# Second-layer values of two heads by seven block products, with their weight sums made ahead and the value step one head later

## The chip, the cores and the metric

One core of one Trainium2 chip runs the whole program once. The metric is the device time of one execution in microseconds (us), taken as the median of the runs shown. All matmuls run on TensorE (PE). VectorE (DVE) and ScalarE (ACT) evict and transform, GpSimd (POOL) does a few additions and issues the transfers of the prepared weights, SyncE (SP) issues most other transfers. PSUM holds eight banks, four for products (`mmt`) and four for everything else (`axt`).

## The reference

Two decoder layers over 528 tokens (16 learned ones and 512 real ones) of width 1024. The first layer is an mLSTM with an RG-LRU, the second differential attention; each is followed by a squared-ReLU MLP of width 4096. The change is in the second layer's attention:

```python
def _diff_attn(hn, w_in, lam_vecs, subln, w_out, lambda_init):
    q, k, v = _split(hn @ w_in, C_SPLITS)       # 8 heads; q, k: 2 x 64 each, v: 128
    ...
    q = _partial_rope(q, cos, sin) * (C_QK_DIM ** -0.5)
    k = _partial_rope(k, cos, sin)
    ...
def _diff_attend(qb, q_pos, kh, vh, k_pos, lam):
    s = jnp.einsum('bhcqd,bhckd->bhcqk', qb, kh)
    p = jax.nn.softmax(jnp.where(mask, s, -jnp.inf), axis=-1)
    pd = p[:, :, 0] - lam * p[:, :, 1]
    return jnp.einsum('bhqk,bhkv->bhqv', pd, vh)
```

Here `hn` is the RMS-normed residual; each head's output is normed again over its 128 columns and goes through `w_out`.

## The kernel before

Activations lie with the features on the partitions and the 528 tokens along the free dimension, cut into eight k blocks of 128 features. Every fp32 operand is split into a high and a low half (`split`: ACT rounds, DVE subtracts), and each product is made of three matmuls: high by high, low by high, high by low. A weight unit is 128 x 1024, eight blocks of 128 x 128. A full product of a unit is 48 matmuls of 264 columns (two banks), or 24 of 512 columns (one bank) where only the real tokens are wanted (`unit_mm`, `cuts`).

The MLPs already make some products in the way that the change brings to the values: `pair_mm` takes two weight units and two token halves as a 2 x 2 by 2 x 2 block product with seven instead of eight block products, on sums of weight blocks (`sums`, `rest`) and of input blocks (`pair_x`). Its three banks are X, Y and Z.

The second layer runs head by head (`attend`): a query product (512 columns), a key product, a value product, each evicted with the row scale `rstd` that the norm leaves out of its inputs. `norm_x` only multiplies by the norm weights, splits, and squares (`norm_sq`). Between them stand the steps of the earlier head (`attn_steps`): `s0` to `s3` are the scores and softmax of four query blocks, `t0` to `t3` the transposes of the probabilities, `v` the transposes of the values into token-major form, `o` the product of probabilities and values, `f` the norm of the head's output into `co`. `SLOTS` is an order written out by hand: slot 0 stands ahead of a head's query product, 1 in its middle, 2 after it, 3 and 4 the same for the key, 5 in the middle of the value product; a prime means one head further back. The framework then schedules all instructions on its engines' queues by that order as priority (`soon` and `now` raise it) and by what is ready, so instructions of several steps and products interleave; it also places the tiles in memory by their lifetimes.

After the last head, the out-projection first multiplies heads 0 to 5 and then heads 6 and 7 (`OUT_K`), with the last heads' steps between its blocks.

The second layer's weights (`AHEAD`: 24 units of query, key and value, 8 of the out-projection) are prepared during the first MLP: `make_ahead` runs every five steps of that MLP's 225 (`STAGE`), fetches half units into `ra` through POOL's queue, splits them two turns later and stores the halves in DRAM (`parts`). In the second layer `emit_load` loads them with SP into three buffers (tag `w`).

## Time and profile before

| | |
|---|---|
| median of 3 runs (lowest to highest) | 1402.62 us (1402.36 to 1403.05) |
| the profiled execution, its span | 1402.5 us, 1400.6 us |
| first layer up to its MLP | 0 to about 444 us |
| first MLP | to 799.5 us |
| second layer's heads | 800 to 990 us |
| out-projection and last heads' steps | 990 to 1048 us |
| second MLP and the output | to 1400.6 us |

A row of the table of stretches gives, for each engine, busy us and the number of instructions, then the granted TensorE clock as a share of full speed (1.00 throughout these stretches), the mean share of the 16 DMA engines and GB/s. A row of the timeline or of the chain that ended last gives the start, the duration and what ran; in brackets stands how long the engine was idle before it, and what ended that. A row of the groups gives busy us and the mean ns of one, and the idle time ahead of them.

### The profile page before, as it was taken

To read this page: it belongs to the slowest core of one execution; us is meant where nothing else is said; L and a number is where in the kernel's file an instruction comes from. 1 tells how busy PE (TensorE), PEld (TensorE's weight loads), DVE (VectorE), ACT (ScalarE), POOL (GpSimd) and SP (SyncE) were. 2 spreads that over 40 slices of the span, in tenths; PEclk is the share of its full clock that TensorE was granted. 3 is DMA by queue.
4 is the path that set the end of the run, shared out by engine and by line. 5 is a ranking of instruction groups with operands and counts; after the bars stand their busy time and mean duration, and the time that the engine had idled before them with its cause. 6 is when DMAs were issued, how large, how long until landed. Compare 5 with 4: busy or idle time off the path is not lost.

```text
span 1400.6 us, 25665 instructions
## 1 busy us (share of the span) xinstructions
PE 1391.1 (99%) x10195; PEld 1324.6 (95%) x10195; DVE 1014.5 (72%) x1836; ACT 764.5 (55%) x1345; POOL 178.7 (13%) x270
## 2 busy tenths in 40 slices
PE   9999999999999999999999999999999999999998
PEld 9999999999999999999999999999887889889986
DVE  6867764757845998888886457878778977777752
ACT  7465844647524565656554336566666554454542
POOL 3000001010012034345430300000011000000001
PEclk9999999999999999999999999999999999999999
DMA  7342324223224369889872266555442333233231
GB/s 227 127 121 84 90 76 128 67 71 105 76 91 129 100 234 355 302 312 318 304 266 85 113 218 198 176 181 166 153 164 65 134 118 118 75 110 105 76 121 45
DMA packets 70068, 210.18 MB, mean 150 GB/s; under 512 B 12570, under 2 KB 14631, under 8 KB 69948
## 3 DMA queue, kind: packets, MB, share of 16 engines
q1 hardware_dynamic: 52732, 154.98, 34.6%
q0 software_dynamic: 15360, 50.34, 9.7%
q10 hardware_dynamic: 1856, 3.21, 0.7%
q8 instruction: 80, 1.31, 0.4%
q14 instruction: 40, 0.33, 0.1%
HBM read 162.11 MB, written 35.71 MB: 141 GB/s over the span
## 4 chain that ended last, share of the span: by engine, by line
PE 80%; ACT 1%; DVE 0%; issue 0%; ACTq 0%
PE mw L997 23%; PE mm L426 21%; PE mpY L345 8%; PE mpX L345 5%; PE mpZ L345 5%; PE mn L997 4%; PE mf L1342 3%; PE mo L1306 3%; PE po L1266 2%; PE pt L1242 1%; PE mm L440 1%; PE psc L1208 1%; PE psc L1207 1%; PE pnum L718 1%; PE pv L1188 0%; PE pss L694 0%
## 5 line engine op out<-in xcount | busy, mean ns | idle before, releaser
L241 ACT CAST wh<-raw 128x1024 fp32r<-128x1024 f32 x139 | 145.4, 1048 | 258.6 <-PE mw L997 82.0
L997 PE MATMUL mw<-al,wh 128*128 128x264 f32 (+1 forms) x704 | 221.2, 314 | 0.0
L997 PE MATMUL mw<-ah,wh 128*128 128x264 f32 (+1 forms) x704 | 221.0, 314 | 0.0
L997 PE MATMUL mw<-ah,wl 128*128 128x264 f32 (+1 forms) x704 | 220.9, 314 | 0.0
L162 DVE TENSOR_TENSOR wl<-raw,wh 128x1024 fp32r<-128x1024 f32 (+1 forms) x138 | 164.5, 1193 | 52.1 <-ACT wh L241 50.2
L997 PEld LDWEIGHTS mw<-ah,wl 128*128 128x128 f32 x704 | 132.4, 188 | 8.3
L997 PEld LDWEIGHTS mw<-ah,wh 128*128 128x128 f32 x704 | 132.4, 188 | 7.3
L997 PEld LDWEIGHTS mw<-al,wh 128*128 128x128 f32 x704 | 132.3, 188 | 7.3
L1041 DVE TENSOR_TENSOR h<-mw,h 128x264 f32<-128x264 f32 (+1 forms) x176 | 87.4, 497 | 22.0 <-PE mw L997 21.5
L521 POOL TENSOR_TENSOR nsq<-nsq 128x528 f32<-128x528 f32 (+1 forms) x28 | 42.2, 1508 | 356.0 <-ACT nsq L519 355.5
L345 PE MATMUL mpX<-xp,A_h 128*128 128x264 f32 (+1 forms) x416 | 77.3, 283 | 0.0
L345 PEld LDWEIGHTS mpX<-xp,A_h 128*128 128x128 f32 x416 | 65.1, 188 | 1.1
L345 PE MATMUL mpX<-xp,A_l 128*128 128x264 f32 (+1 forms) x208 | 58.9, 283 | 0.0
L162 DVE TENSOR_TENSOR al<-rt,ah 128x528 fp32r<-128x528 f32 (+1 forms) x64 | 46.0, 719 | 17.1 <-ACT ah L165 16.5
L280 ACT CAST S_h<-sums 128x1024 fp32r<-128x1024 f32 x26 | 27.3, 1051 | 38.3 <-issue 12.6
L1355 POOL TENSOR_TENSOR zg<-z,gfr 128x512 f32<-128x512 f32 x4 | 5.2, 1294 | 328.2 <-DVE z L1349 328.2
L1007 ACT ACTIVATE rt<-rt 128x528 f32<-128x528 f32 (+1 forms) x64 | 40.7, 638 | 9.9 <-DVE rt L1028 8.7
L162 DVE TENSOR_TENSOR ral<-ra,rah 128x512 fp32r<-128x512 f32 x64 | 43.7, 682 | 2.6 <-DMA ra<-wu 1.3
L1220 ACT ACTIVATE e<-e,mx 128x144 f32<-128x144 f32 (+3 forms) x64 | 32.8, 513 | 20.0 <-DVE mx L1212 19.7
L165 ACT CAST ah<-rt 128x528 fp32r<-128x528 f32 (+1 forms) x64 | 40.1, 626 | 1.5
L352 DVE TENSOR_TENSOR hh<-mpZ,hh 128x264 f32<-128x264 f32 (+1 forms) x52 | 22.1, 426 | 25.7 <-PE mpZ L345 25.6
L165 ACT CAST rah<-ra 128x512 fp32r<-128x512 f32 x64 | 37.9, 613 | 3.0 <-DMA ra<-wu 2.8
(941 smaller groups left out, 4378.3 us busy)
## 6 DMA issues: line engine op xcount, KB each, us to landing
raw<-wu SPq DMA_DIRECT2D x139, 512.0 KB, 3.6
rawp<-wu SPq DMA_DIRECT2D x26, 1024.0 KB, 6.4
ra<-wu POOLq DMA_DIRECT2D x64, 256.0 KB, 5.6
h<-hT SPq DMA_DIRECT2D x15, 264.0 KB, 4.9
st<-rh SPq DMA_DIRECT2D x16, 132.0 KB, 4.1
st<-rh ACTq DMA_DIRECT2D x16, 132.0 KB, 4.2
kz<-rl SPq DMA_DIRECT2D x16, 132.0 KB, 5.5
st<-rh SPq DMA_DIRECT2D x16, 128.0 KB, 3.6
```

Of the source, the lines that this page charges most:

```text
L162: eng.tensor_tensor(out=o, in0=a, in1=b, op=ALU.subtract)
L165: nc.scalar.copy(hl[0][:, sl], src)
L241: nc.scalar.copy(wh, raw)
L345: nc.tensor.matmul(st[b][:, :hv], ww[:, cc], xx, start=st[b, "n"] == 0, stop=k == 3 and j == 2, skip_group_check=True)
L426: nc.tensor.matmul(p[:, :m], w[:, c], xx[:, s:s + m], start=(k == 0 and j == 0), stop=(k == KB - 1 and j == len(terms) - 1))
L521: state["kz"] = nc.gpsimd.tensor_tensor(out=fin[0][:, lo:], in0=fin[0][:, lo:], in1=sq[:, lo:], op=ALU.add)
L997: nc.tensor.matmul(ps, w[ww], x[xx][:, tk], start=k == j == 0, stop=k == len(ws) - 1 and j == 2)
L1007: nc.scalar.activation(out=t[:, cols], in_=t[:, cols], func=AF.Square)
L1041: nc.vector.tensor_tensor(out=hf, in0=ps, in1=hf, op=ALU.add)
L1220: nc.scalar.activation(out=e[:, s0:s0 + m], in_=e[:, s0:nk] if last else d[:, :m], func=AF.Exp, scale=-1.0 if last else 1.0, bias=top, acc ...
L1306: nc.tensor.matmul(ps, w[ww][:, b], co[k][xx][:, NM:], start=(k == ks[0] and j == 0), stop=(k == ks[-1] and j == 2))
L1342: nc.tensor.matmul(pss[n][:, :m], a[k][aa][:, tk], w[k][ww][:, f0:f0 + m], start=(k == 0 and i == 0), stop=(k == KB - 1 and i == 2))
```

## The change

The values of two heads are made together, as in the MLPs: seven block products on the two units' blocks and the two token halves. The even head makes four of them (a copy of the first product, two sums, and the first half of its own values), the odd head three. The even head's values are complete only in the odd head, so the step `v` moves one head later; `SLOTS` becomes four orders, for the first two heads, even and odd heads, and the end. The row scale moves from the eviction of the product to the value transposes (`rsV`, rstd transposed through DRAM).

`norm_pairs` takes the place of `norm_x` and also makes the input sums. The blocks lie apart in memory now, so a query product is cut into 248 and 264 columns (two banks).

The weight sums are made in `make_ahead`: 76 half units are split instead of 64 and 16 sums are added; up to two jobs a turn, stores issued in the same turn, `STAGE` up to step 218. The loads move to four buffers shared with the MLP (tag `v`). Besides, small constants move into one tile, one explicit activation table preload is dropped, and in the last recurrent pair a squaring moves from DVE to ACT.

```diff
-SLOTS = ("t2' s0", '', "t1' t3'", '', "o'", "s2 s1 v f' s3 t0")
+SLOTS = (("t2' s1'", '', "v' t3'", "t1' s0 o' t0", '', "s2 s3 f'"),
+         ("t2' s1'", 's0', "t3'", "v' s2 t1' o' t0", '', "f' s3"),
+         ("s1' t2' s0", '', "v' t3'", "t1' o'", 't0', "s2 f' s3"),
+         ("s1' s0", "t2'", "t3'", "v' t1' o'", 's2 t0', "f' s3"))
...
-STAGE = set(range(8, 184, 5))
+STAGE = set(range(8, 220, 5))
...
+        for _u in AHEAD:
+            if _u in V_PAIR:
+                jobs += [("s2", _u), ("s3", _u), ("a0", _u), ("a1", _u), ("s0", _u), ("s1", _u), ("d", _u)]
+            elif all(_u - _p not in (1, 4, 5) for _p in V_PAIR):
+                jobs += [(0, _u), (1, _u)]
...
-            cuts = [(lo, n)] if n <= 512 else [(0, HV), (HV, HV)]
+            cuts = [(lo, n)] if n <= 512 and not isinstance(x[0][0], tuple) else [(lo, HV - lo), (HV, HV)]
...
+            def even(mid):
...
+                ps = product("X", A, 0, B11)
+                with soon():
+                    nc.scalar.copy(h["a"], ps)
+                ps = product("Y", S, 1, N2)
+                with soon():
+                    nc.vector.tensor_tensor(out=h["b"], in0=ps, in1=h["a"], op=ALU.add)
+                mid()
+                ps = product("Z", S, 0, N1)
+                with soon():
+                    nc.vector.tensor_tensor(out=h["c"], in0=ps, in1=h["b"], op=ALU.add)
+                ps = product("X", A, 1, B21)
+                with soon():
+                    nc.scalar.copy(v[0][:, s1], ps)
...
+            def odd(mid):
...
+                ps = product("Y", U, 0, T3)
+                with soon():
+                    nc.vector.scalar_tensor_tensor(out=v[1][:, s2], in0=ps, scalar=-1.0, in1=h["c"], op0=ALU.mult,
+                                                   op1=ALU.subtract)
+                ps = product("Z", U, 1, B22, mid)
+                with soon():
+                    nc.vector.tensor_tensor(out=v[0][:, s2], in0=ps, in1=h["c"], op=ALU.add)
+                ps = product("Y", D, 0, T4)
...
+        def norm_pairs(h, gc):
...
+                for o, hh, g, m in ((n1, h[:, k, :HV], pc(gc + k), b12), (t3, h[:, k + 1, HV:], pc(gc + k + 1), b12),
+                                    (n2, h[:, k, :HV], gneg[:, k:k + 1], t3), (t4, h[:, k + 1, :HV], gneg[:, k + 1:k + 2], n2)):
+                    nc.vector.scalar_tensor_tensor(out=o, in0=hh, scalar=g, in1=m, op0=ALU.mult, op1=ALU.subtract)
+                for o, m in ((hi.a[:, 4:7], b[:, 0:3]), (hi.b, t4)):
+                    nc.scalar.copy(o, m)
+                for o, m, i in ((lo.a[:, 4:7], b[:, 0:3], hi.a[:, 4:7]), (lo.b, t4, hi.b)):
+                    sub(nc.vector, o, m, i.bitcast(F32))
...
-                    if pr == 3:
-                        nc.vector.tensor_tensor(out=d["a2"], in0=d["a"], in1=d["a"], op=ALU.mult)
-                    else:
-                        nc.scalar.activation(out=d["a2"], in_=d["a"], func=AF.Square)
+                    nc.scalar.activation(out=d["a2"], in_=d["a"], func=AF.Square)
...
-            vr = sc("vr1")
-            steps.append(attn_steps(hd, rot, vr))
-            ps = unit_mm(u + 2, x, mid=lambda: slot(hd, 5))
-            with soon():
-                for p, tk in ps:
-                    nc.vector.tensor_tensor(out=vr[:, tk], in0=p, in1=rstd[:, tk], op=ALU.mult)
+            mid = lambda: slot(hd, 5)
+            if hd % 2 == 0:
+                vals.append(values_in_pairs(u_qkv(hd, 2), xp))
+                steps.append(attn_steps(hd, rot, vals[-1][0][0]))
+                vals[-1][1](mid)
+            else:
+                steps.append(attn_steps(hd, rot, vals[-1][0][1]))
+                vals[-1][2](mid)
...
+                    for j, (s0, sz) in enumerate(KBLK):
+                        i, c = j // 4, slice((j % 4) * P, (j % 4 + 1) * P)
+                        nc.scalar.activation(out=vt[0][i][:sz, c], in_=pvs[i][:sz, c], func=AF.Copy, scale=rsV[:sz, j:j + 1])
+                        nc.vector.scalar_tensor_tensor(out=vt[1][i][:sz, c], in0=pvs[i][:sz, c], scalar=rsV[:sz, j:j + 1],
+                                                       in1=vt[0][i][:sz, c].bitcast(F32), op0=ALU.mult, op1=ALU.subtract)
```

More of the change, by code (lines that the diff above doesn't have):

```diff
@@ L39, with u_qkv, __init__, at @@
 U_QKV = 129
-U_OUT1 = 153
-U_MLP1 = 161
-N_UNIT = 225
+U_OUT1 = 161
+U_MLP1 = 169
+N_UNIT = 233
+def u_qkv(hd, w):
+    return U_QKV + 8 * (hd // 2) + 4 * (hd % 2) + w
+V_PAIR = [u_qkv(hd, 2) for hd in range(0, 8, 2)]
+class Blocks:
+    def __init__(self, a, b):
+        self.a, self.b = a, b
+    def at(self, i):
+        return self.a[:, i, :] if i < 7 else self.b
 PLAN = """
@@ L57 @@
 N_S = 31
-AHEAD = range(129, 161)
+AHEAD = range(U_QKV, U_MLP1)
 N_W = 4
@@ new lines, in trunk, with half, job, add @@
+        n_job = [0]
+        got, made, sums = {}, [], {}
+        def half(c):
+            return slice(c * 512, c * 512 + 512)
+        def job(j, u):
+            if j in (0, 1):
+                return got.pop((u, j))[1], u, j
+            r = {v: got[u, v][1] for v in range(4) if (u, v) in got}
+            def add(k, a, b):
+                o = sc("rs_")[:, :512]
+                nc.vector.tensor_tensor(out=o, in0=a, in1=b, op=ALU.add)
+                if k > 1:
+                    sums[u, k] = o
+                return o
+            if j == "s2":
+                return add(2, r[3], r[2]), u + 1, 0
+            if j == "s3":
+                return add(3, sums.pop((u, 2)), r[0]), u + 1, 1
+            if j == "a0":
+                return r[0], u, 0
+            if j == "a1":
+                return got.pop((u, 1))[1], u, 1
+            if j == "s0":
+                del got[u, 0], got[u, 2]
+                return add(0, r[0], r[2]), u + 4, 0
+            if j == "s1":
+                return add(1, sums.pop((u, 3)), state.pop(("r1", u))), u + 4, 1
+            return got.pop((u, 3))[1], u + 5, 0
@@ L255, in make_ahead, with here @@
         def make_ahead():
             state["turn"] = state.get("turn", 0) + 1
+            def here(j, u):
+                need = {"s2": (2, 3), "s3": (0,), "a1": (1,)}.get(j, (j,) if j in (0, 1) else ())
+                return all((u, v) in got and got[u, v][0] <= state["turn"] - LAG for v in need)
+            n = 0
+            while jobs and n < 2 and here(*jobs[0]):
+                j, u = jobs.pop(0)
+                if j == "a1":
+                    state["r1", u] = got[u, 1][1]
+                raw, to, c = job(j, u)
+                hl = sc("rah", F32R), sc("ral", F32R)
+                split(hl, raw, slice(0, 512))
+                made.extend((part[:, half(c)], t) for part, t in zip(parts[to - AHEAD[0]], hl))
+                n += 1 if j in (0, 1) else PJOB
@@ L260, in make_ahead @@
                 nc.gpsimd.dma_start(out=part, in_=t[:, :512].bitcast(F32))
-            while came and came[0][0] <= state["turn"] - LAG:
-                _, i, c, raw = came.pop(0)
-                hl = sc("rah", F32R), sc("ral", F32R)
-                split(hl, raw, slice(0, 512))
-                made.extend((part[:, c], t) for part, t in zip(parts[i - AHEAD[0]], hl))
-            if ahead:
-                i = ahead.pop(0)
-                for c in (slice(0, 512), slice(512, 1024)):
+            for _ in range(2):
+                if fetch and len(got) < CAP:
+                    u, v, src, c = fetch.pop(0)
                     raw = sc("ra")[:, :512]
-                    nc.gpsimd.dma_start(out=raw, in_=wu[seq[i]][:, c])
-                    came.append((state["turn"], i, c, raw))
+                    nc.gpsimd.dma_start(out=raw, in_=wu[seq[src]][:, half(c)])
+                    got[u, v] = (state["turn"], raw)
         todo = []
@@ L843, in out_gate @@
             nc.scalar.activation(out=so[c], in_=so[c], func=AF.Sigmoid)
-        sp = cp.tile([P, 8], F32, name="sp")
-        spn = cp.tile([P, 8], F32, name="spn")
+        sp = small(8)
+        spn = small(8)
         def lru_consts():
@@ L1074, in trunk @@
         mlp(0, 0, "m", between)
-        while ahead or came or made:
+        while jobs or made:
             make_ahead()
-        assert not (ahead or came or made)
+        assert not (jobs or made or got or sums)
         dump("h2", h)
-        x, terms1 = norm_x(h, C_NMIX1, 0, "d")
-        tb = [sc(f"tb{i}") for i in range(2)]
+        xp, terms1 = norm_pairs(h, C_NMIX1)
+        xq = [tuple((t, o) for t in hl) for hl in xp for o in (0, 2)]
+        tb4 = big.tile([P, 2, T], F32, tag="tb", name="tb", bufs=1)
+        tb = [tb4[:, i] for i in range(2)]
+        vals = []
+        rrow2 = dr.tile([1, T], F32, name="rrow2")
+        rsV = small(5)
         for i in range(2):
-            nc.sync.dma_start(out=tb[i], in_=rope[i])
+            load(tb[i], rope[i])
         lvt = cp.tile([1, 4, 64], F32, name="lvt")
@@ L1119, in slot @@
         def slot(hd, i):
-            for s in SLOTS[i].split():
+            for s in SLOTS[0 if hd < 2 else 1 if hd > 7 else 2 + hd % 2][i].split():
                 g = hd - 1 - s.count("'")
```

127 lines of the change are left out of this document (98 added, 29 removed).

## The prediction

> **What bounds the kernel now.** I read the page's busy shares first, then the table of stretches, then the chain that ended last, then single instructions. In the fences the first number of a timeline or chain row is its start in us.
>
> ```profile
> span 1400.6 us, 25665 instructions
> PE 1391.1 (99%) x10195; PEld 1324.6 (95%) x10195; DVE 1014.5 (72%) x1836; ACT 764.5 (55%) x1345; POOL 178.7 (13%) x270
> core 0: us, PE busy (x) PEld busy (x) DVE busy (x) ACT busy (x) POOL busy (x), PEclk, DMA share, GB/s
> 460.00:799.50 339.50, 339.50 (x2789) 339.50 (x2788) 278.40 (x444) 187.52 (x278) 111.51 (x196) 1.00 0.71 246
> 862.00:887.40 25.40, 25.40 (x180) 23.75 (x179) 20.23 (x63) 16.22 (x47) 0.00 (x0) 1.00 0.56 175
> 887.40:912.70 25.30, 25.30 (x177) 23.33 (x176) 21.04 (x67) 17.00 (x48) 0.00 (x0) 1.00 0.60 183
> 473.75 5.83 PE mw L997 x48
> 1077.56 5.55 PE mw L997 x24
> 1111.34 1.42 PE mpY L345 x12
> ```
>
> PE is busy everywhere, and a busy PE need not be PE at its pace, so I took the pace from runs of one shape in the chain: 48 matmuls of 264 columns in 5.83 us are 121.5 ns each, 24 of 512 columns 231.3 ns, 12 of 256 columns 118.3 ns. The first MLP holds 2789 matmuls, nearly all of 264 columns; 339.50/2789 is 121.7 ns. So that stage has no stall to give back. One head of the second layer (862.0 to 887.4, and the next) takes 25.3 to 25.4 us with PE at its pace and DVE at 80 to 83%. The time is PE's instruction stream, and what counts is how many columns it streams and whether the new side work ever makes it wait.
>
> **The change, part by part.**
>
> *Value products.* Two heads' values take 2 x 48 matmuls of 264 columns now; seven block products of 4 x 3 take 84. Four pairs lose 48: 48 x 121.5 ns = -5.83 us, all on PE.
>
> *Query products.* With the inputs cut into blocks, a query product of 24 matmuls of 512 columns becomes 24 of 248 and 24 of 264, in eight heads: 192 more instructions. From 256 and 512 columns the slope is (231.3 - 118.3)/256 = 0.441 ns per column and the rest 5.3 ns, so 248 columns cost an estimated 114.8 ns. The split costs 114.8 + 121.5 - 231.3 = 5.0 ns, times 192 = +0.96 us. The fixed part could be larger where small instructions mix. The nearest other row is this:
>
> ```profile
> 863.95 0.71 PE L1188 MATMUL pv<-keep,vr 128*72 128x128 f32 x5
> 864.42 0.48 PE L426 MATMUL mm<-dx2l,wh 128*128 128x512 f32 x1
> ```
>
> Five transposes of 128 columns take 0.47 us to the next start, 94 ns each, 38 ns over the slope. At 38 ns the split would cost 7.3 us; at none, 0. I take 5.0 ns, since the new matmuls are of the kind of the 256-column rows and no transposes. [...]
>
> *Weight sums in the first MLP.* By the code's lists 64 half-unit splits become 76 and 16 sums are added; 128 stores from POOL become 152, the 64 fetches stay.
>
> ```profile
> L162 DVE TENSOR_TENSOR ral<-ra,rah 128x512 fp32r<-128x512 f32 x64 | 43.7, 682 | 2.6 <-DMA ra<-wu 1.3
> L165 ACT CAST rah<-ra 128x512 fp32r<-128x512 f32 x64 | 37.9, 613 | 3.0 <-DMA ra<-wu 2.8
> 502.26 0.68 DVE L301 TENSOR_TENSOR sums<-sums,rawp 128x512 f32<-128x512 f32 x1
> L270 POOL DMA_DIRECT2D ra<-wu x64 | 34.7, 545 | 25.3 <-DVE al L162 17.7 <-DMA part141h<-rah 1.4 <-DMA part156h<-rah 1.1
> 500.00:520.00 20.00, 20.00 (x166) 20.00 (x166) 18.80 (x30) 12.50 (x20) 6.02 (x12) 1.00 0.68 223
> 740.00:760.00 20.00, 20.00 (x167) 20.00 (x166) 11.59 (x21) 8.64 (x12) 0.00 (x0) 1.00 0.18 53
> ```
>
> DVE gets 12 x 0.682 + 16 x 0.68 = 19.1 us, ACT 12 x 0.613 = 7.4, POOL 24 x 0.545 = 13.1. Over the stage DVE goes from 82% to 88%, ACT from 55% to 57%, POOL from 33% to 37%. The turns now run from step 8 to 208 of 225 instead of to about 178, into the stretch after 740 where DVE stands at 58% and DMA at 0.18. In the crowded stretch (94% at 500 to 520) a turn on a value pair can hold 1.4 us more, but those splits have the low priority and no PE instruction waits for them before 800. I take 0. If that cover is gone, one such turn shows as a stall of its 1.4 us, and there are some eight such turns.
>
> *The norm before layer two.* Per pair of k blocks it adds on DVE four 264-column operations and two subtractions (792 and 264 columns), on ACT three.
>
> ```profile
> 801.00 0.77 DVE L485 SCALAR_TENSOR_TENSOR dx7l<-h,keep,dx7h 128x528 fp32r<-128x528 f32 x1 [0.74 <-ACT dx7h L483]
> 810.56 0.71 DVE L470 SCALAR_TENSOR_TENSOR rqa<-rqa,nv 128x528 f32<-128x528 f32 x1 [8.79 <-ACT rqa L469]
> 805.85 0.60 ACT L1138 ACTIVATE qs<-mm 128x512 f32<-128x512 f32 x1 [4.34 <-PE mm L426]
> L1175 DVE TENSOR_TENSOR vr<-mm,drstd 128x264 f32<-128x264 f32 x14 | 5.4, 424 | 0.0
> ```
>
> At 0.42 us for 264 columns (L1175) the four are 1.7 us; 1056 columns of subtraction at 0.682 us for 512 are 1.4; four pairs make 12.4 us on DVE. ACT copies 1320 columns a pair at 0.613 us for 512, 1.6 us, in all 6.4. The last residual block is split at 801.00, so three of the four pairs can start before 800; DVE is idle 8.79 us ahead of 810.56 and ACT 4.34 us ahead of 805.85; and the first value product comes after query and key, 24 x 231.3 + 48 x 121.5 ns = 11.4 us of PE. Only its second product reads a new block. I take 0; uncovered, the last pair's share of 3 us. The six small DMAs for the transposed rstd stand on SP's queue once, behind rstd at 812; weights of the next head queue behind them with some 6 us to spare. Price 0.
>
> *Attention.* A pair of heads loses four scalings of values (L1175) and gains five combining operations on DVE and two copies on ACT; each head's value transposes are evicted in five pieces instead of three, each query in two instead of one.
>
> ```profile
> L162 DVE TENSOR_TENSOR v1l<-pv,v1h 128x256 fp32r<-128x256 f32 x6 | 2.5, 416 | 0.5 <-ACT v1h L1191 0.5
> L162 DVE TENSOR_TENSOR v1l<-pv,v1h 72x256 fp32r<-72x256 f32 x6 | 2.5, 413 | 0.0
> L162 DVE TENSOR_TENSOR v1l<-pv,v1h 128x128 fp32r<-128x128 f32 x6 | 1.7, 288 | 0.5
> L1147 DVE SCALAR_TENSOR_TENSOR qr<-mm,tb 128x512 f32<-128x512 f32 x7 | 4.8, 681 | 1.0 <-ACT qs L1138 1.0
> 861.85 0.41 PE L426 MATMUL mm<-dx7h,wl 128*128 128x264 f32 x2
> 869.90 0.29 PE L426 MATMUL mm<-dx0h,wh 128*128 128x264 f32 x1
> 870.93 0.76 DVE L1175 TENSOR_TENSOR vr<-mm,drstd 128x264 f32<-128x264 f32 x2
> 872.09 0.33 PE L426 MATMUL mm<-dx0h,wh 128*128 128x264 f32 x1
> ```
>
> DVE: one more combining operation, 0.42 us per pair; evictions 5 x 0.288 = 1.44 for 0.416 + 0.413 + 0.288 = 1.12 now; queries 2 x 0.42 for 0.68. Together about +0.7 us per head, 84 to 88% of a head shortened to 24.7 us. Weight loads per pair rise from 6 to 7.5 MB, with DMA at 0.56 now. An even head's value products hold three of the four product banks instead of two, and a query needs two instead of one. The last four rows show what a late bank does now: values finished at about 862.2 are evicted at 870.93, and the next product's second bank opens at 872.09; meanwhile PE runs the first bank alone from 869.90 and loses nothing. I take 0, upper bound 1 us per pair.
>
> *Elsewhere.* In the last recurrent pair a squaring moves from DVE to ACT, twice, on this chain:
>
> ```profile
> 343.03 0.74 ACT L926 ACTIVATE ri<-ri,spn 128x528 f32<-128x528 f32 x1
> 345.08 1.18 ACT L934 ACTIVATE a<-a 128x528 f32<-128x528 f32 x2
> 350.72 0.51 PE L426 MATMUL mm<-yb6h,wh 128*128 128x264 f32 x2 [1.06 <-ACT yb6h L165]
> ```
>
> Two squarings, at the 1.18 us that two square roots take, delay those roots by up to 1.2 us, and PE already waits 1.06 us for what follows. Below nothing is possible too, since DVE no longer does the two multiplications, were DVE the later one; but the roots wait for ACT's own queue here. Between 0 (other matmuls go first) and +1.2 I take +0.5. The dropped table preload only moves a load; 0.
>
> The tail is the tightest cover. Head 6 now brings its values and one softmax step into it, at most some 3 us of DVE and ACT:
>
> ```profile
> 1034.75 0.62 ACT L165 CAST co7h<-rqy 128x512 fp32r<-128x512 f32 x1 [2.75 <-DVE rqy L1283]
> 1037.67 0.39 PE L1306 MATMUL mo<-co7h,wh 128*128 128x512 f32 x1
> 1005.00:1010.00 5.00, 5.00 (x28) 4.42 (x28) 1.77 (x5) 1.38 (x4) 0.00 (x0) 1.00 0.53 185
> ```
>
> Head 7's output is cast at 1035.4 and wanted at 1037.7, a slack of 2.3 us (1.6 with the low part), plus the 1 us of PE work that moves in too, and DVE idles 3.2 us of 1005 to 1010. Price 0, upper bound 2.
>
> **Sum.** -5.83 + 0.96 + 0.5 = -4.4 us. The profiled execution took 1402.5 us, 1.9 over its span and 0.1 under the median of 1402.62. 1402.5 - 4.4 is 1398.1; I say 1398.2.
>
> **Rivals.**
>
> 1. *The covers in attention leak* (same). Banks at 1 us per pair cost 4 us: 1402.1. With half of that and 1 us of tail, 1401.1. For it: the eviction 8.7 us late at 870.93, and five banks asked of four. Against it: PE's stand-in work in the same rows.
> 2. *DVE becomes the bound of a head* (slower). If the 83% of 887.4 to 912.7 (21.04 of 25.30) were the most that the softmax chains let DVE reach, a head with 21.04 + 0.7 us would take 26.1 instead of 25.3; eight heads lose 6.7 us and the saving on PE is not collected: 1402.5 + 6.7 + 0.5 = 1409.7. It decides once the ceiling lies under 86% (21.7/25.3). Against it: 94% at 500 to 520 with PE at its pace.
> 3. *Splitting the queries costs a fixed price per matmul* (same): at 38 ns the sum is -5.8 + 7.3 + 0.5 = +2.0, 1404.5. [...]
>
> **How the numbers follow.** This kernel's three times spread over 0.05%; 0.2% is 2.8 us, about what can be told from no change, so "same" is 1399.8 to 1405.4. Forecast 0.62 (1396.5 to 1399.7, the low end with no query cost and a better order around 350), rival 1 0.25, rival 2 0.10, rival 3 0.03. Faster 0.62, same 0.28, slower 0.10. A range from 1396.5 to 1402.5 takes in the forecast and nearly all of rival 1.
>
> **What would show it.** PE should have 10195 - 48 + 192 matmuls; two heads should take 49.5 us instead of 50.7; the first MLP should stay at 121.7 ns a matmul with DVE near 88%; PE should wait nowhere between 800 and 1048. The prediction is wrong if PE shows gaps ahead of a query or ahead of the second product into a held bank, if heads stay at 25.3 us with DVE above 86%, if the out-projection waits for head 7, or if the 248-column matmuls are spaced wider than 115 ns.

## The result, and the profile after

The changed kernel takes 1417.93 us (median; 1416.92 to 1420.81) against 1402.84 us (1402.36 to 1403.39) for the kernel before on the same chip: a ratio of 1.0111, 95% interval 1.0099 to 1.0123. It is slower by 15.1 us, where 4.4 us less was forecast. The page of its profiled execution:

```profile
span 1416.5 us, 26167 instructions
PE 1395.3 (98%) x10339; PEld 1332.6 (94%) x10339; DVE 1048.2 (74%) x1914; ACT 786.6 (56%) x1403; POOL 193.1 (14%) x294
PE 81%; DVE 8%; ACT 5%; DMA 3%; issue 1%; POOL 1%; SPq 1%; ACTq 0%; DVEq 0%; POOLq 0%
```

TensorE has 10339 matmuls, 10195 - 48 + 192, as forecast. The last line is the chain that ended last; that of the kernel before was

```profile
PE 80%; ACT 1%; DVE 0%; issue 0%; ACTq 0%
```

So the chain now runs through DVE for 8%, ACT for 5% and DMA for 3%: PE waits. The starts of four landmarks on PE show where (us):

| | before | after | difference |
|---|---|---|---|
| to the first matmul of the first MLP | 443.9 | 445.3 | +1.4 |
| first MLP | 355.6 | 357.3 | +1.8 |
| from its last matmul to the first of the second MLP | 248.7 | 262.5 | +13.8 |
| second MLP | 298.5 | 297.4 | -1.1 |
| the rest | 54.0 | 54.0 | 0 |

The last matmul before the second layer starts at 799.44 us before and at 802.63 after. Busy time by stretch, of the kernel before (the first 20 us of the second layer, the next 20, a pair of heads), then of the changed kernel (the first MLP, the same two stretches, two pairs of heads):

```profile
799.50:819.50 20.00, 20.00 (x134) 18.42 (x134) 9.34 (x18) 7.05 (x12) 5.05 (x8) 1.00 0.35 119
819.50:839.50 20.00, 20.00 (x138) 18.74 (x137) 11.55 (x34) 5.68 (x16) 0.00 (x0) 1.00 0.83 252
862.00:912.70 50.70, 50.70 (x354) 47.08 (x353) 41.27 (x127) 33.22 (x95) 0.00 (x0) 1.00 0.58 179
```

```profile
core 0: us, PE busy (x) PEld busy (x) DVE busy (x) ACT busy (x) POOL busy (x), PEclk, DMA share, GB/s
461.40:802.60 341.20, 339.62 (x2789) 339.41 (x2788) 299.74 (x483) 194.58 (x295) 123.27 (x220) 1.00 0.75 264
802.60:822.60 20.00, 18.01 (x139) 17.10 (x138) 15.74 (x25) 10.09 (x18) 7.29 (x9) 1.00 0.40 142
822.60:842.60 20.00, 16.82 (x123) 16.31 (x122) 10.45 (x27) 5.59 (x15) 0.00 (x0) 0.91 0.86 241
874.40:927.80 53.40, 51.48 (x389) 48.37 (x388) 42.57 (x131) 35.56 (x103) 0.00 (x0) 1.00 0.61 198
927.80:981.10 53.30, 51.47 (x391) 48.46 (x390) 42.58 (x132) 35.74 (x103) 0.00 (x0) 1.00 0.62 199
```

PE was busy for every microsecond of these stretches before. Now it loses 2.0 us in the first 20, 3.2 in the next, and 1.8 to 1.9 in each pair, which takes 53.3 to 53.4 us in place of 50.7, with DVE at 80% (42.57 of 53.40) in place of 81%. A busy PE also counts some slow spacing (four matmuls of 264 columns from 838.31 on take 220 ns each at a busy share of 1.00), so from here I use the *excess*: for each row of PE's timeline, the time to the next start less 0.4414 ns a column and 5.3 ns a matmul (the pace of the prediction). Summed over 20 us each from the last matmul of the first MLP on, it is 0.9, 0.4, 1.6, 1.3, 1.1 ... us before and 3.7, 5.8, 2.1, 2.0, 2.7 ... after. These are sums over one profiled execution of each kernel.

The waits themselves, on PE's timeline of the changed kernel:

```profile
806.10 0.64 PE L509 MATMUL mm<-xq,wh 128*128 128x248 f32 x4
806.57 0.40 PE L509 MATMUL mm<-xq,wl 128*128 128x248 f32 x2
806.81 0.64 PE L509 MATMUL mm<-xq,wh 128*128 128x248 f32 x4
809.64 0.50 PE L509 MATMUL mm<-xq,wh 128*128 128x248 f32 x2 [1.24 <-ACT xq L671]
810.45 0.50 PE L509 MATMUL mm<-xq,wh 128*128 128x248 f32 x2 [0.30 <-DVE xq L672]
811.63 1.16 PE L709 MATMUL nps<-nsq,keep 128*128 128x264 f32 x4 [0.45 <-POOL nsq L695]
835.22 0.31 PE L1384 MATMUL psc<-st,st 128*128 128x144 f32 x1 [2.10 <-DMA st<-rh]
835.83 0.30 PE L1385 MATMUL psc<-kz,st 128*128 128x144 f32 x1 [0.31 <-DMA kz<-rl]
836.91 0.30 PE L1384 MATMUL psc<-st,st 128*128 128x144 f32 x1 [0.77 <-DMA keep<-rrow]
838.31 1.08 PE L509 MATMUL mm<-xq,wh 128*128 128x264 f32 x4
839.19 0.65 PE L509 MATMUL mm<-xq,wl 128*128 128x264 f32 x2
876.82 0.40 PE L1384 MATMUL psc<-st,st 128*128 128x272 f32 x1 [0.67 <-ACT e L1397]
900.24 0.51 PE L530 MATMUL vpY<-xq,wh 128*128 128x264 f32 x2 [0.33 <-DVE vr L558]
905.06 0.34 PE L1384 MATMUL psc<-st,st 128*128 128x144 f32 x1 [0.39 <-ACT e L1397]
909.94 0.74 PE L1419 MATMUL pt<-keep,e 128*72 128x128 f32 x5 [0.20 <-DVE e L1408]
910.96 0.51 PE L509 MATMUL mm<-xq,wh 128*128 128x264 f32 x2 [0.28 <-DVE qr L1320]
```

Three groups. At 809 to 812 the query product waits for the last residual blocks (the normed tiles of lines 671 and 672), and the norm's own product (`nps`) for POOL's sum of squares. At 835 to 837 the first score matmuls wait for transfers, two of their operands and one, by the profile, of the row scale. From 876 on, waits of 0.2 to 0.7 us come back in each pair of heads: score matmuls for exponentials, the second product into bank Y for the eviction of the first, a key product for the eviction of a query. Most come again one pair later, at 930, 953.6, 963 and 964 us.

### The profile page after: what moved, and what is told of

Same layout as the page of the kernel before. It is cut to its first block, busy times and chain, and to the rows that moved or that the text cites. A ratio compares the mean times of both kernels' runs of the same rounds, so it can differ in the third digit from the quotient of the medians.

```text
span 1416.5 us, 26167 instructions
## 1 busy us (share of the span) xinstructions
PE 1395.3 (98%) x10339; PEld 1332.6 (94%) x10339; DVE 1048.2 (74%) x1914; ACT 786.6 (56%) x1403; POOL 193.1 (14%) x294
## 4 chain that ended last, share of the span: by engine, by line
PE 81%; DVE 8%; ACT 5%; DMA 3%; issue 1%; POOL 1%; SPq 1%; ACTq 0%; DVEq 0%; POOLq 0%
PE mm L509 23%; PE mw L1163 21%; PE mpY L421 8%; PE mpZ L421 5%; PE mpX L421 5%; PE mn L1163 4%; PE mo L1483 3%; PE mf L1519 3%; DMA raw<-wu 2%; PE po L1443 2%; PE pnum L887 1%; PE pss L863 1%; ACT e L1397 1%; DVE wl L183 1%; PE mm L579 1%
## 5 line engine op out<-in xcount | busy, mean ns | idle before, releaser
L1207 DVE TENSOR_TENSOR h<-mw,h 128x264 f32<-128x264 f32 (+1 forms) x176 | 87.6, 499 | 12.0 <-PE mw L1163 11.3
L509 PE MATMUL mm<-xq,wh 128*128 128x264 f32 (+1 forms) x512 | 90.4, 290 | 2.0 <-ACT xq L671 1.2
L509 PEld LDWEIGHTS mm<-xq,wh 128*128 128x128 f32 x512 | 73.3, 191 | 3.0 <-ACT xq L671 1.5
L509 PE MATMUL mm<-xq,wl 128*128 128x264 f32 (+1 forms) x256 | 53.8, 286 | 0.0
L509 PEld LDWEIGHTS mm<-xq,wl 128*128 128x128 f32 x256 | 41.0, 191 | 0.0
```

Of the source, the lines that this page charges most:

```text
L509: nc.tensor.matmul(p[:, :m], w[:, c], cols_of(xx, s, m), start=(k == 0 and j == 0), stop=(k == KB - 1 and j == len(terms) - 1))
L1207: nc.vector.tensor_tensor(out=hf, in0=ps, in1=hf, op=ALU.add)
```

## Experiments

Times are medians against runs of the kernel before on the same chip (1402.6 to 1403.0 us). The framework reorders instructions and moves tiles with almost every edit, so few edits are quite alone; what each moved is read by stretches, from one profiled execution of each.

**The orders, on the kernel before.** One kernel gets the four new orders with the values one head later, one the late values with the old order, one the new orders with the values where they were:

```diff
 # orders_before: the four new tuples; values_later:
-SLOTS = ("t2' s0", '', "t1' t3'", '', "o'", "s2 s1 v f' s3 t0")
+SLOTS = ("t2' s0", '', "v' t1' t3'", '', "o'", "s2 s1 f' s3 t0")
 # orders_values_here: the four new tuples with v' taken out and v ahead of f' in slot 5
```

> The kernel before with nothing but the four new orders of steps, the values one head later with them. Theory C: two heads take 52.5 to 54 us instead of 50.6 and the time rises 6 to 11 us, to 1409 to 1414. Rival D: two heads stay below 51 us, the time within 2 us of 1402.8, and the orders as such are free.

> The kernel before with one edit: the value step of a head (its transposes and evictions) runs one head later, in slot 2, and the order of all other steps stays as it was; products, MLP sums and evictions are those of before. Theory L (running the values one head later is what cost the 11.3 us that the four new orders cost on the kernel before): 1410 to 1414 us, and waits of PE at psc, pt or poq in 840 to 1050 that the trace of before has not. Theory O (the new places of the score and transpose steps cost it): 1402 to 1404 us, within 0.1% of the 1402.9 of before.

> The kernel before with the four new orders of the score, transpose and output steps, but with the value step left in the last slot of its own head; products, MLP sums and evictions are those of before. Theory O (the new places of the steps cost the 11.3 us): 1410 to 1415 us. Theory L (the values one head later cost them): 1402 to 1404 us. If both share: 1405 to 1409 us.

Measured: 1414.20 us (ratio 1.0081, 1.0066 to 1.0096), 1405.06 (1.0016, 1.0007 to 1.0026) and 1413.28 (1.0076, 1.0060 to 1.0093). Late values alone cost 2.2 us, the new orders alone 10.4. Theory O holds, though 1405.06 lies 1 us above the 1404 that it gave for the late values: on the kernel before, without one block product, the orders cost two thirds of the 15.1 us by which the changed kernel is slower. By the profiles, 1.8 us of the first cost and 1.4 of the last lie ahead of the first MLP, where no moved step runs (its first matmul starts at 445.66 and 445.28 in place of 443.88); between the MLPs the new orders alone cost 9.7 us. The waits of the last run stand late in the stage: its excess reaches 2 us only from 120 us after the MLP on (up to 4.0 in 20 us), with rows like this one of its PE timeline, a score step waiting for VectorE:

```profile
1007.23 0.39 PE L1210 MATMUL psc<-st,st 128*128 128x264 f32 x1 [0.93 <-DVE mx L1215]
```

**Room on VectorE.** In these runs the rotation of queries and keys is left out:

```diff
-                with pri("R"):
-                    nc.vector.stream_shuffle(out=sh[:, lo:], in_=sh[:, lo:], mask=shuf)
-                    pool_or_dve("tT"[w]).tensor_tensor(out=sh[:, lo:], in0=sh[:, lo:], in1=tb[1][:, lo:], op=ALU.mult)
-                    pool_or_dve("rR"[w]).tensor_tensor(out=raw[:, lo:], in0=raw[:, lo:], in1=sh[:, lo:], op=ALU.add)
```

> The kernel before with the rotation left out in the same way: the control. TensorE is full there in both theories: 1399 to 1403 us.

> The kernel before with the four new orders (1414.2 us with the rotation), and the rotation left out in the same way. Theory D: 1400 to 1405 us, the orders cost under 4 us once VectorE has room. Rival P: 1409 to 1414 us.

> The changed kernel with the second layer's rotation of queries and keys left out (its shuffle, product and sum, six instructions and some 4.2 us of VectorE in each head); only the product with the first rope table is left in the computation. Theory D (VectorE's queue, 80% busy in a pair of heads, answers PE late): VectorE falls to 63 to 68%, two steady heads take 51 us or less in place of 53.3, and the time is 1403 to 1409 us. Rival P (the steps stand too close to the scores and exponentials they need, whatever VectorE's load): two steady heads stay at 52.3 us or more, and the time is 1411 to 1417 us.

Measured: 1402.76 us for the control (ratio 1.0000, 0.9990 to 1.0009), 1403.13 with the new orders (1.0002, 0.9993 to 1.0012), and 1420.75 for the changed kernel (1.0125, 1.0109 to 1.0142). On the kernel before theory D's times came: with the rotation gone the orders cost 0.4 us in place of 11.3. The same stretch in the run with the orders, and in that one without the rotation, each with rows of PE from it:

```profile
930.00:983.00 53.00, 51.22 (x345) 46.11 (x344) 39.34 (x117) 31.98 (x92) 0.00 (x0) 1.00 0.54 171
941.40 0.48 PE L1281 MATMUL poq<-osh,keepr 128*128 128x512 f32 x1 [0.66 <-ACT osh L1275]
942.10 0.49 PE L1282 MATMUL poq<-osl,keepr 128*128 128x512 f32 x1 [0.22 <-DVE osl L165]
```

```profile
930.00:983.00 53.00, 52.92 (x371) 49.28 (x371) 35.26 (x110) 35.61 (x98) 0.00 (x0) 1.00 0.55 171
935.69 0.40 PE L1277 MATMUL poq<-osh,keepr 128*128 128x512 f32 x1
```

Theory D's mechanism is not shown by this. DVE's share is no ceiling: 74% (39.34 of 53) goes with waits here, and under the old order 81% (41.27 of 50.7) left PE full. All four waits of the stretch, 1.7 us together, stand at step `f`, the norm of a head's output, which needs what ACT (`osh`) and then DVE (`osl`) make of the product of step `o`; ACT starts on it as soon as that product ends (939.95, after 939.91). PE asks too soon: between `o` and `f` of the fourth to sixth heads stand 6 or 7 matmuls, against 55 to 57 in the kernel before and 41 to 46 in the run without the rotation. So leaving out the rotation did not only unload DVE, it also gave PE another order, and it shortened the way from a product to the score operands. Which of the three removed the cost is not separated. In the run with the values where they were, 37 to 42 matmuls stand in that place and the waits are others, like the one at 1007.23. What the rows do show is that a step waits where it is asked for too soon after its operands.

On the changed kernel D falls, and 1420.75 lies outside rival P's range too: DVE went down to 63 to 67% and the waits only changed their releaser. Rows of its PE timeline:

```profile
902.11 0.27 PE L1381 MATMUL psc<-kz,st 128*128 128x144 f32 x1
905.39 0.46 PE L1380 MATMUL psc<-st,st 128*128 128x144 f32 x1 [3.01 <-DMA wl<-part148l]
906.17 1.07 PE L509 MATMUL mm<-xq,wh 128*128 128x248 f32 x4
907.04 0.64 PE L509 MATMUL mm<-xq,wl 128*128 128x248 f32 x2
```

The score step now waits longer for transfers: 2.34 us at 961.94 for st<-rh, and 3.01 us here, which the profile puts down to a weight load that the step does not read; the last part of its own `st` had been issued at 898.16, 7.2 us ahead of the step's start at 905.39, and its landing is not in the trace. After the wait four matmuls take 0.87 us. So two further runs set the score steps later as well:

```diff
 # no_rotation_spread: even and odd heads, besides the rotation
-         ("s1' t2' s0", '', "v' t3'", "t1' o'", 't0', "s2 f' s3"),
-         ("s1' s0", "t2'", "t3'", "v' t1' o'", 's2 t0', "f' s3"))
+         ("s1' t2'", 's0', "v' t3'", "t1' o'", 's2 t0', "f' s3"),
+         ("s1'", "s0 t2'", "t3'", "v' t1' o'", 's2 t0', "f' s3"))
 # no_rotation_all: also, for the first two heads, and the block sums behind the norm's root
-SLOTS = (("t2' s1'", '', "v' t3'", "t1' s0 o' t0", '', "s2 s3 f'"),
+SLOTS = (("t2' s1'", '', "v' t3'", "t1' o'", 's0 t0', "s2 s3 f'"),
```

> The changed kernel without the rotation (left out as in the run of that name) and with the score steps set apart as in the run with the scores spread. Theory T (two chains bind in turn: VectorE's queue, and the transfers of a head's score operands, which land about 7 us after their issue; a step set 3 us later clears the second once the first has room): two steady heads take 50 to 51.5 us, no wait for a transfer of over 0.5 us in 876 to 985, and the time is 1404 to 1411 us. Rival U (the shorter products leave too little of TensorE's work between any steps): two steady heads stay at 53 us or more, 1415 to 1425 us.

> As the run beside it, and also with the first score step of head 0 in slot 4 and the second layer's block sums after the norm's root. Theory T: below that run by 2 to 5 us, 1400 to 1408 us. Rival U: 1415 to 1425 us.

Measured: 1419.25 us (1.0119, 1.0102 to 1.0136) and 1423.92 (1.0153, 1.0138 to 1.0168). Theory T fell. In the first the long waits for transfers are gone from the pairs of heads (0.35 us is left), but others stand in their place:

```profile
876.80 0.39 PE L1380 MATMUL psc<-st,st 128*128 128x272 f32 x1 [0.99 <-DVE mx L1385]
904.55 0.63 PE L1415 MATMUL pt<-keep,e 128*72 128x128 f32 x4 [1.18 <-DVE mx L1385]
```

Two heads took 53 to 54 us, with DVE at 69 to 70%: rival U's numbers. (In the second of these runs the block sums did not move, as is shown for `late_blocks` below.) That TensorE then arrives too early for its own four score banks fits the code (`axp` has four), but which limit it is was not shown.

**The score operands' queue.** The transfers that build `st` and `kz` go through POOL's queue:

```diff
 # and kz's nc.sync likewise
-                    eng = nc.scalar if w and c else nc.sync
+                    eng = nc.gpsimd
```

> The changed kernel with the transfers that build the score operands of a head (st from rh and rl, kz from rl) issued on POOL's queue in place of SP's and ACT's; the whole computation is kept. Theory F (they stand behind weight loads of 512 KB on SP's queue, so the first score step waits 2.10 us for st<-rh): the excess of the second 20 us after the MLP falls from 5.8 us to 3 us or less, 1412 to 1415 us. Rival (what they wait for is the norm's late root, 7 us later than before, and the 16 DMA engines that all queues share): 1416 to 1420 us.

Measured: 1449.79 us (1.0337, 1.0322 to 1.0353), outside both. From issue to landing these transfers took, in the changed kernel's page and then between 870 and 985 us of this run:

```profile
st<-rh SPq DMA_DIRECT2D x16, 132.0 KB, 3.8
kz<-rl SPq DMA_DIRECT2D x16, 132.0 KB, 4.2
```

```profile
st<-rh POOLq DMA_DIRECT2D x16, 132.0 KB, 5.2
kz<-rl POOLq DMA_DIRECT2D x8, 132.0 KB, 6.7
```

Landing 1.4 and 2.5 us later went with 32 us over the changed kernel. Not all of that is waiting: the granted clock was 0.90 from 870 to 985 us. This fits orders in which the score steps have little slack against their transfers. Theory F's remedy failed; SP's queue as the cause was not separated from the load on the DMA engines (of the 16 engines' time between 870 and 985 us of this run, the packets of SP's queue took 39.5% and those of POOL's 17.0%).

**The norm and the first score step.** Four runs on the changed kernel: block sums meant to stand after the root; POOL's seven additions replaced by fills; the row scale a constant; the first score step later.

```diff
 # late_blocks: the block sums of norm_pairs become blocks(k), called behind the scaling of tb
+                    for k in range(0, KB, 2):
+                        blocks(k)
 # writes_only, this norm alone: the sum over k blocks is left out
-                state["kz"] = nc.gpsimd.tensor_tensor(out=fin[0][:, lo:], in0=fin[0][:, lo:], in1=sq[:, lo:], op=ALU.add)
+                state["kz"] = nc.gpsimd.memset(fin[0][:, lo:], 100.0)
 # constant_scale: the six transfers by way of rrow2 go, and
+        nc.vector.memset(rsV, 1.0)
 # first_score_later: the order of the first two heads as in no_rotation_all
```

> The changed kernel, with the block sums of the norm ahead of layer two (the second loop of norm_pairs) emitted behind the row scale and the scaled rope tables, so that they rank behind the plain splits and behind the chain that makes rstd. In the changed kernel PE waits 3 us at 808 to 812 for those splits and 5 us at 832 to 843 for head 0's rotated queries and keys, whose scale comes 7 us later than before. Theory A (order in the norm): both waits go, the first query of head 1 stands some 18.5 us after that of head 0 instead of 21.2, and 43 to 45 us later stands that of head 3 instead of 50; the time falls 7 to 9 us, to about 1409 to 1411. Rival (the work itself is too much, in whatever order): the waits move to the first value product, which needs the sums, and the time stays within 2 us of 1418.

> The changed kernel; in the norm ahead of layer two POOL's seven additions of squares (two SBUF inputs, 1.3 to 1.6 us each) are replaced by fills of the same tile, which read nothing; the sum over k blocks is left out there. In the changed kernel a DVE instruction with two SBUF inputs that starts beside such an addition lasts about 1.1 us longer (1.87 for 0.77 us). Theory B (POOL's additions hold DVE up): no DVE instruction of 783 to 814 is longer than its kind elsewhere, DVE gets through the norm 5 to 7 us earlier, the wait at 808 to 812 goes or shrinks below 1 us, and the time falls 4 to 8 us. Rival (DVE has simply too many instructions there): DVE's instructions keep their lengths, and the time stays within 2 us of 1418.

> The changed kernel with the row scale of the values replaced by a constant 1.0, filled once: the transfer of the norm's row to memory and the five transfers back are gone, and the row scale of the second layer's values is left out of the computation. Everything else stays. Theory R (these transfers, and the waits on the tile that they write, feed the stall of 832 to 837 us, where a score matmul waited 0.77 us for keep<-rrow and the granted clock fell to 0.88 after it): 1411 to 1415 us, and the excess of the second 20 us after the MLP falls from 5.8 us to under 3.5 us. Rival (the stall follows the late norm, whose reciprocal root comes 7 us later than before, and the wait for st<-rh of 2.10 us stays): 1416 to 1418 us.

> The changed kernel with one edit in the order of the first two heads: the first score step of head 0 and its transposes stand after the key product of head 1 (slot 4) in place of inside it (slot 3), 3 us later. Theory S (the stall of 832 to 837 us is a score step that stands ahead of the transfers it needs, which landed at 835 to 837 us): the excess of the second 20 us after the MLP falls from 5.8 us to 3 us or less, the granted clock stays at 1.00 there, and the time is 1412 to 1415 us. Rival (the wait only moves to the next step, as it did in the run with fills in place of the additions): the first four stretches sum to 13 us or more as before (13.6 us), 1416 to 1419 us.

Measured: 1416.56 us (1.0100, 1.0083 to 1.0117), 1414.80 (1.0087, 1.0071 to 1.0103), 1418.09 (1.0112, 1.0089 to 1.0134), 1419.69 (1.0127, 1.0104 to 1.0150). The excess of the first three stretches, and the time from the first MLP to the second:

| | 1st | 2nd | 3rd | sum | MLP to MLP |
|---|---|---|---|---|---|
| changed kernel | 3.7 | 5.8 | 2.1 | 11.6 | 262.5 |
| late_blocks | 5.3 | 2.8 | 3.2 | 11.3 | 261.9 |
| writes_only | 0.9 | 3.2 | 7.2 | 11.3 | 261.8 |
| constant_scale | 3.7 | 5.8 | 2.3 | 11.8 | 262.4 |
| first_score_later | 4.9 | 2.4 | 5.0 | 12.3 | 262.7 |

`late_blocks` moved nothing that matters: in its trace PE, ACT and POOL run the same instructions in the same order as in the changed kernel, and on DVE one copy of a single column stands elsewhere. All sixteen block sums still start ahead of the root, within 0.1 us of where they did, counted from the MLP's last matmul. So theory A was not tested, in this run or in the two that carry the same edit (no_rotation_all, spread_and_late). The row is a second look at one order, and it shows what the table can tell: the first and second stretch differ by 1.6 and 3.0 us between two executions of the same order (3.7 and 5.8, 5.3 and 2.8), and the sum by 0.3. One profile of each is too little to credit an edit with a stretch.

The row scale's transfers cost nothing: constant_scale is the changed kernel within its spread, with score waits of 1.66, 0.35 and 1.00 us in the same place, and theory R fell. In `first_score_later` (1419.69) theory S fell too: the waits moved, as its rival said, and the first four stretches sum to 14 us.

`writes_only` is a clean edit: the order on PE, DVE and ACT is that of the changed kernel, and only POOL's seven additions are replaced. The first stretch is as clean as before (0.9), and the root `drstd` is made 12.0 us after the last matmul of the MLP, as before (11.9), in place of 15.8. The fills also take the sum out of the chain to the root, but that is not what brought it forward: the last square, which ACT makes ahead of the last addition, starts 1.6 us after the MLP's last matmul in place of 6.9, and the norm's product at 6.3 leaves room for an addition of 1.3 us. So it is POOL's additions, by way of the VectorE operations that they lengthen, that hold up the norm's end. The time falls by 3.1 us, less than theory B's 4 to 8 and hardly clear of the spread, for the score steps wait next: the first 60 us of the profiled execution, the slowest of its four, lose 11 us all the same.

**Other edits of the changed kernel.** One order for all heads (that of values_later); the values evicted in three pieces; the score steps set apart; that with the first score later and late blocks; the query uncut.

```diff
 # three_pieces, without the row scale
+                    for (i, sz, c) in ((0, 72, slice(0, 256)), (0, P, slice(256, 512)), (1, P, slice(0, P))):
+                        nc.scalar.copy(vt[0][i][:sz, c], pvs[i][:sz, c])
+                        sub(nc.vector, vt[1][i][:sz, c], pvs[i][:sz, c], vt[0][i][:sz, c].bitcast(F32))
 # query_whole, besides N_S = 29
-            cuts = [(lo, n)] if n <= 512 and not isinstance(x[0][0], tuple) else [(lo, HV - lo), (HV, HV)]
+            cuts = [(lo, n)] if n <= 512 else [(0, HV), (HV, HV)]
```

> The changed kernel with one order of steps for all heads, that of the kernel before with the values one head later: t2' s0 ahead of the query, v' t1' t3' after it, o' after the key, s2 s1 f' s3 t0 inside the value product. Theory C (the four new orders cost the heads' 2.7 us per pair): two heads take 49.5 to 51 us instead of 53.3, and the time falls 5 to 9 us. Rival D (the heads carry more work on DVE and ACT and a query needs two banks, in whatever order): two heads stay at 52.5 to 54 us and the time within 2 us of 1418.

> The changed kernel with the values evicted in three pieces in each of the two parts, as before, in place of five, and without the row scale and its six transfers: the row scale of the second layer's values is left out of the computation. Four instructions fewer in each head (two on ACT, two on DVE). Theory E (the longer evictions hold a PSUM bank and VectorE, and so make the waits of two steady heads, 3.7 us in each pair, at psc for ACT e and at mm for DVE qr): 1406 to 1412 us and two steady heads in 50 to 51.5 us in place of 53.3. Rival (the waits come from where the steps stand in the order): two steady heads stay at 52.5 to 53.5 us, and the time is that of the run with a constant scale within 2 us.

> The changed kernel with the score steps set apart in the orders of even and odd heads: s0 moves from slot 0 to slot 1, s2 of even heads from slot 5 to slot 4; nothing else is edited. Theory S (three score steps stand within 6 us at a head's boundary, and the second waits for the exponentials of the first: 0.83 us at 876.82, 0.72 at 905.06, 0.85 at 930.31): these waits for ACT e go, two steady heads take 51.0 to 52.3 us in place of 53.3, and the time is 1411 to 1415 us. Rival (ACT and DVE are too full for the shorter products, and the waits turn up elsewhere): two steady heads stay at 53 to 54 us, 1416 to 1420 us.

> The changed kernel with three edits together: the first score step later (as in the run of that name), the score steps set apart, and the second layer's block sums after the norm's reciprocal root (as in the run with late blocks, which took 1416.6). Theory S, with the three gains adding up (1.4, 3.5 and 4.5 us below 1417.9): 1407 to 1410 us. Rival (waits move rather than go): 1414 to 1419 us.

> The changed kernel with the query product uncut: one matmul of 512 columns into one PSUM bank in place of two of 248 and 264 columns into two, 192 matmuls fewer; to make room, 29 buffers of 512 columns in place of 31 serve the work tiles. Theory Q (the cut costs 1 us as matmuls, and its second bank costs the waits at mm for DVE qr, 0.66 us in each pair of heads): 1413.5 to 1416 us and no wait for DVE qr of over 0.2 us. Rival (the cut costs its matmuls alone): 1416.5 to 1418 us.

Measured: 1426.63 us (1.0163, 1.0148 to 1.0179), 1423.79 (1.0149, 1.0134 to 1.0164), 1424.16 (1.0156, 1.0139 to 1.0173), 1426.36 (1.0174, 1.0157 to 1.0191), 1441.33 (1.0272, 1.0256 to 1.0287). All are worse than the changed kernel, and all lie above both of the times that were expected of them. The old order with late values costs 2.2 us with eight products and loses by 23.7 with seven, so it is not the new orders as such that fail there. Four evictions fewer in each head (three_pieces) brought score steps ahead of their transfers (a wait of 1.81 us for st<-rh at 879). Setting the scores apart shrank the waits at 876 and 930 from 0.8 to 0.2 us of excess, as theory S said, but put 2.2 us before a key product at 884 and 1.5 before the value transposes at 910. query_whole tells nothing of the query: its 29 buffers already cost 8.6 us ahead of the first MLP.

## Why the prediction was wrong

The failed step is the overlap: the price 0 for attention, "upper bound 1 us per pair", and the price 0 for the norm. Between the MLPs 262.5 us pass, where 248.7 less the 4.9 of products and cut makes 243.8. Of the 18.7 us lost, 8.2 are excess of the first 40 us (the norm's end and head 0's first scores: 9.5 in place of 1.3), and about 10.5 fall in the rest. Two heads were to take 49.5 us; they take 53.3 to 53.4, 3.8 more. The work was forecast right: DVE is busy for 42.6 us in a pair, where 41.27 and twice 0.7 make 42.7. What the prediction had wrong is that PE would find each step ready when its turn came.

And the four orders had no term in the sum at all: I took the products' cost and the added side work apart, and treated the moved steps as neutral as long as each engine had room. On a kernel that is otherwise the one before, the orders cost 10.4 us, or 11.3 with the late values. That the changed kernel pays this same amount for them is not shown: there the old order with late values is slower still (one_order), and leaving out the rotation, which took the cost away on the kernel before, gains nothing.

A division by steps, from the profiles: from orders_before to the changed kernel the profiled span grows from 1413.2 to 1416.5, by 3.3 us, where products and cut should give -4.9. The excess of the first two stretches grows from 1.3 to 9.5 us (+8.2), the other stretches to the second MLP by 2.8, the first MLP by 2.1 (355.2 to 357.3), and the second MLP is 4.6 us shorter (302.0 to 297.4; in orders_before its first products start among the last heads' steps and wait 1.81 us at 1060.53, so this too is the orders' cost): +8.2 + 2.8 + 2.1 - 4.6 - 4.9 = +3.6; the 0.3 left over lie ahead of the first MLP.

- *Value products*: right. 48 matmuls fewer, at the pace given; by their number and pace the saving is there, and waits eat it.
- *Query cut*: right. Six matmuls of 248 and 264 columns from 806.10 to 806.81 are 118.3 ns each, the mean of 114.8 and 121.5. So rival 3 is out. But a gap came behind it, 0.28 us at 910.96: the key product waits for the eviction of a query (`qr`), which needs two banks now.
- *Weight sums*: DVE reached 87.8% (299.74 of 341.20) for the 88% forecast. The cover mostly held: the first MLP takes 355.2 to 355.8 us in six kernels without the sums and 355.5 to 357.8 in the fourteen that have the code of the sums, 0 to 2 us. In the profile of the changed kernel one stall makes most of it, about the 1.4 us that the prediction named as the sign, where DVE has no idle time:

```profile
690.00:700.00 10.00, 8.43 (x69) 8.21 (x68) 10.00 (x16) 5.12 (x8) 3.74 (x7) 1.00 0.38 119
697.38 0.51 PE L421 MATMUL mpY<-xp,U_h 128*128 128x264 f32 x2 [1.57 <-DVE hh L428]
```

- *The norm*: wrong. "I take 0; uncovered, 3 us": the first stretch lost 2.8 us. I counted DVE's and ACT's own work and left out POOL's additions beside it; they were in the kernel before too, but there the only DVE operations that started beside them were those of line 1041, which read one input from PSUM and kept their 0.43 us. The root came at 818.46 in place of 811.31, 4.0 us of it made in this stretch, and with it the score operands, 5.4 us in the second stretch. DVE and POOL in the changed kernel:

```profile
806.59 1.60 POOL L695 TENSOR_TENSOR nsq<-nsq 128x528 f32<-128x528 f32 x1 [2.81 <-ACT nsq L693]
806.92 1.56 DVE L183 TENSOR_TENSOR xq<-xc,xq 128x264 fp32r<-128x264 f32 x1
808.74 0.88 DVE L683 SCALAR_TENSOR_TENSOR xc<-h,keep,xd 128x264 f32<-128x264 f32 x2
810.31 2.09 DVE L683 SCALAR_TENSOR_TENSOR xc<-h,keep,xc 128x264 f32<-128x264 f32 x2
810.27 1.31 POOL L695 TENSOR_TENSOR nsq<-nsq 128x528 f32<-128x528 f32 x1 [2.08 <-ACT nsq L693]
818.46 0.71 DVE L611 SCALAR_TENSOR_TENSOR drstd<-rqa,rqy 128x528 f32<-128x528 f32 x1
```

- *Six small DMAs at 0*: right (constant_scale).
- *Squaring at +0.5*: PE waits 0.86 us for it at 352.91 in place of 1.06, and the changed kernel is 1.1 us behind both at 307 and at 354: net 0. *Table preload at 0*: the load stands 1.7 us later (89.36 for 87.61) and PE waits 0.31 us at 91.97; a landmark at 112 is 0.7 us further behind than one at 87.
- *The tail at 0*: right; from 1020 to 1065 no wait of PE is recorded, and the second MLP follows at once.
- *Rival 1* was right in kind and, for the banks, in size: the second product into Y (0.33 us of waiting at 900.24) and the key product (0.28 at 910.96) have 1.0 us of excess together in that pair, and 0.9 in the next. That was also one of the prediction's own signs of being wrong. Score steps and transposes that wait for the softmax make most of the rest.
- *Rival 2* had the sign but not the mechanism, and its 1409.7 lies 8 us short. There is no ceiling at 83%: DVE fell to 80% and PE still waited.

What stays open: why no order that was tried brings the seven products to the pace of the eight. Three kinds of releaser are seen (VectorE's queue, the transfers of the score operands, banks held by ACT or VectorE); in the runs where one kind shrank, another stood in its place. What sets the pace of the steady heads is not shown. No version that beats the kernel before was found.

## What to carry over

An order of steps written by hand is part of the kernel's cost: price a reordering by the time between each step and the slowest of what it needs (eviction, transfer, exponentials), and try it alone, on the old kernel, before the new arithmetic. Where PE is full, shortening its work can take cover from the steps behind it; here the 48 matmuls that went brought no time back (two heads took 53.3 to 53.4 us, 50.7 before). A wait can go from one stretch and come back in the next, with an edit or, as in late_blocks, without a change of order, so judge an edit by the sum over stretches and by more than one execution. And compare the order of instructions on each engine before and after an edit: late_blocks left it as it was, and leaving out the rotation, meant to unload one engine, changed it on another.

## What the hardware showed

*VectorE's operations last longer beside POOL's additions.* In the fence above the two operations of line 683 take 0.88 us for two at 808.74 and 2.09 at 810.31, beside POOL's addition of 810.27 to 811.58; the subtraction of 264 columns at 806.92 takes 1.56 us beside the one of 806.59, where one at 790.20 took 0.42 with none beside it. The same at 793.67, where one operation took 1.87 us instead of 0.77 beside an addition from 793.64 on. The operation with one input in PSUM kept its length: 0.43 us at 791.77, beside the addition of 791.73 to 793.05, and 0.43 at 782.47 with none beside it. With fills in place of the additions no VectorE operation around the norm is longer than its kind; the same two pairs in writes_only:

```profile
804.08 0.89 DVE L684 SCALAR_TENSOR_TENSOR xc<-h,keep,xd 128x264 f32<-128x264 f32 x2
805.65 1.01 DVE L684 SCALAR_TENSOR_TENSOR xc<-h,keep,xc 128x264 f32<-128x264 f32 x2
```

The pair that took 2.09 us beside an addition takes 1.01 here. What in the hardware lengthens the operations, no run shows.

*A wait can cost more than its length.* After the stall of 832.7 to 837 four matmuls of 264 columns take 0.88 us (838.31 to 839.19), 220 ns each where 121.5 is the pace, with a granted clock of 0.50 from 838.31 to 840.95 and 0.91 over the stretch. The waits ahead of them are 2.1, 0.3 and 0.8 us, with single matmuls between them. In late_blocks the slow pace came behind the norm, after waits of 1.24, 0.30 and 0.44 us, at a granted clock of 0.69 from 808 to 813 us (the two matmuls from 812.20 to 812.64 take 220 ns each):

```profile
809.63 1.89 PE L709 MATMUL nps<-nsq,keep 128*128 128x264 f32 x4 [0.44 <-POOL nsq L695]
812.20 0.64 PE L509 MATMUL mm<-xq,wl 128*128 128x264 f32 x2
812.64 0.96 PE L509 MATMUL mm<-xq,wh 128*128 128x264 f32 x4
```

Yet the same three waits in the changed kernel (1.24, 0.30 and 0.45 us, 809 to 812) left the clock at 1.00, and behind the score waits of late_blocks (0.74 and 0.95 us) the pace was full (the second stretch lost 2.8 us there, 5.8 in the changed kernel). The order of the instructions was the same in both, so it does not decide where the slow pace falls; in the first stretch, with the same waits, this alone makes 1.6 us (5.3 against 3.7). How long a wait brings the slow pace is not shown.
